# Copies of the strided score operands by GpSimd in a dilated attention layer, with the low part of the probabilities stored over the scores

## The chip, the cores and the metric

The kernel runs on one core of a Trainium2 chip. A core has five engines that run side by side, each in the order of its own instruction stream: TensorE (PE, with its weight loads as PEld), VectorE (DVE), ScalarE (ACT), GpSimd (POOL) and SyncE (SP). They meet at semaphores. DMA transfers are issued from the streams of SP, ACT and POOL. The metric is the device time of one execution in microseconds; less is better. The profile shows one execution with the time of each instruction.

## The reference, cut to what matters

The program is a trunk of two residual layers on 2048 tokens of 1024 columns. The first (even) layer has forgetting attention and gated linear attention, the second (odd) layer retention and dilated attention. Only the dilated attention of the odd layer is touched. It has eight heads of 64 columns, and each head is computed at three dilations:

```python
DIL_PATTERNS = ((128, 1), (512, 4), (2048, 16))

def _dilated_branch(q, k, v, window, dil):
    span = window // dil
    ...
    qs = to_strided(q)                  # tokens t, t + dil, ... in blocks of 128
    kb = with_prev(to_strided(k))       # a block and the one before it
    vb = with_prev(to_strided(v))
    s = jnp.einsum('bhrnqd,bhrnkd->bhrnqk', qs, kb, preferred_element_type=F32) * dh ** -0.5
    valid = (rel >= 0) & (rel <= span) & (...)
    s = jnp.where(valid, s, -jnp.inf)
    mx = jnp.max(s, axis=-1, keepdims=True)
    p = jnp.exp(s - mx)
    den = jnp.sum(p, axis=-1, keepdims=True)
    o = jnp.einsum('bhrnqk,bhrnkd->bhrnqd', p, vb.astype(F32)) / den
    lse = (mx + jnp.log(den))[..., 0]
```

With dilation 4 the query at t sees t, t - 4, ..., t - 512. With dilation 16 there are 128 tokens in each residue class, so there is one block and none before it. The outputs at the three dilations are mixed by a softmax of their lse.

## The kernel before

Every fp32 operand is kept as two fp16 parts. A head's queries and keys lie in one tile st of 128 partitions x 3 x 2048 tokens: column blocks [q_hi; q_lo], [k_hi; k_hi] and [k_lo; k_lo], so that two matmuls give the whole product of a query block and a key block. Tokens are consecutive in the free direction. A residue class at dilation 4 or 16 is therefore a slice with step 4 or 16 (8 or 32 bytes), used directly as a matmul's operands: slice(512 * b + r, 512 * b + 512, 4) or slice(r, S, 16).

A head has 12 groups of four units; a unit is a query block of 128 tokens with its keys. Groups 0 to 3 are dilation 1 (pattern 0), groups 4 to 7 are dilation 4 (pattern 1, group 4 + b is the block b of 512 tokens with the four residues), groups 8 to 11 are dilation 16 (pattern 2, four residues each). They run in the order 4 to 11, then 0 to 3. A unit has 256 keys where there is a block before it, and 128 otherwise (always in pattern 2).

The function scores works on one group. TensorE makes eight matmuls (lines 873 and 874) into one of two PSUM tiles big. VectorE scales, masks and takes the row maximum of each unit into the fp32 tile raw, named dl_s (line 876, line 879), ScalarE takes the exponential with the row sum (line 880), then rounds the whole group to fp16 as ph (line 882). VectorE subtracts and writes the rest as fp16 pl (line 883). SyncE issues two transposing DMAs, ph and pl into the tile pt (lines 884 and 885). Tiles dl_s, dl_ph, dl_pl and dl_pt have two buffers each. The function values, two groups later (LAG = 2), makes the products of pt with the values (lines 895 and 896) into aux, and ScalarE and VectorE add them up (lines 899 and 902).

Between these steps TensorE makes the projections: those of the next head (Heads.tiles: 48 matmuls of 192 columns through the helper rows, lines 163 to 165, into one of two PSUM tiles dn) and others that are stored to memory (Extra.rows, 256 columns). A projection of the next head is rotated by VectorE (lines 743 to 746) and GpSimd (line 747, the sum), and rounded by ScalarE (line 402 for q and k, line 403 for v) and VectorE (lines 405 and 407). Every four row tiles, SyncE transposes q and k into st of the next head (line 413). GpSimd stores the other projections (x_out, line 233), sends the results of patterns 1 and 2 through memory to put the tokens in their order (rec_d, lines 909 and 910), and loads v in the order of the patterns (lines 840 to 844). Weights are split into two parts by ScalarE and VectorE (lines 82 and 83).

The lists of steps are merged by costs written in the code (merge, periods). A planner then sets each engine's order by a simulated timeline (schedule_with_timeline_sim=True), in which an instruction waits for its buffers. So engine order is not always the order of the text.

Of the kernel before, what the change touches and what calls it, by code (L numbers as in the profile page):

```python
# [7 lines left out]
F32 = mybir.dt.float32  # L8
# [9 lines left out]
S = 2048  # L18
# [7 lines left out]
GLA_BUFS = 2  # rows that a recurrence may run ahead of the output products  # L26
RET_BUFS = 3
RET_ROWS = 3  # rows of retention next to the last of the other products
SHARE1, REST1 = 120.0, 20.0  # products left for the last head's attention, and for after it
SHARE2, REST2 = 80.0, 40.0  # L30
LAG = 2  # steps from scores to values
LAG_EVEN, LAG_ODD = 2, 2  # row tiles from the output's operands to its products


class Core:
    """Tools that both layers share: norms, weights in two fp16 parts, products."""
# [24 lines left out]
    def pow2_scale(self, s, inv, ssq):  # L61
        """Powers of two s and inv = 1 / s with sqrt(ssq) * s < 2**14.5."""
# [7 lines left out]
    def rstd(self, ssq, n, shift, k=1):  # L70
        """2**shift / sqrt(ssq / n + EPS)"""
# [8 lines left out]
    def split(self, hi, lo, x, scale):  # L80
        """hi + lo = x * scale"""
        self.nc.scalar.activation(hi, x, AF.Copy, scale=scale)  # L82
        self.nc.vector.scalar_tensor_tensor(lo, x, scale, hi, op0=OP.mult, op1=OP.subtract)  # L83
# [4 lines left out]
    def put_u(self, u, t, h, work):  # L88
        """Row tile t of the normed stream, split and transposed."""
# [15 lines left out]
    def begin_w(self, into, key, *args):  # L105
        """Load a weight now, and leave the rest of its work to finish_w."""
# [9 lines left out]
    def start_w(self, w, segs, gain, pool=None, space=None):  # L116
        """Columns of a weight times the gain of their rows, in two fp16 parts, and the scale's inverse."""
# [37 lines left out]
    def rows(self, out, u, t, w, c0, c1):  # L155
        """out[token, column] = u[tile t] @ w[:, c0:c1]"""
# [10 lines left out]
    def cols(self, out, u, b, w, c0, c1):  # L167
        """out[column, token] of a block of 512 tokens"""
# [9 lines left out]
def merge(main, fill):  # L178
    """Emit two lists of (cost, unit), the second spread evenly over the first."""
# [13 lines left out]
def take(units, cost):  # L193
    """The first units that come to about a cost, taken off their list."""
# [7 lines left out]
class Extra:  # L202
    """Products that go to memory: silu's two factors, and the operands of the recurrent heads."""
# [16 lines left out]
    def rows(self, n, t, k, store):  # L220
        """Row tiles t and t + 1 of 256 columns."""
# [13 lines left out]
    def cols(self, n, b, c, k, store):  # L235
        """128 columns of a block of 512 tokens."""
# [7 lines left out]
    def units(self, gate0, gate_d, after, rows=(), cols=()):  # L244
        """cols: ((first columns, stores, shifts) of two times 128 columns); rows: (first column, store).
        after: weights to load for later."""
# [31 lines left out]
class Recurrent:  # L278
    """The steps of recurrent heads in their order, and the rows that they made."""
# [921 lines left out]
```

## Time and profile before

| | |
|---|---|
| median of 3 runs | 2428.81 us (2408.69, 2428.81, 2563.56) |
| span of the profiled execution | 2434.8 us |
| busy: TensorE, VectorE, ScalarE, GpSimd | 2208.3, 1579.2, 1166.1, 493.0 us |
| mean granted TensorE clock | 0.955 |
| groups of dilated scores | 96, from 1320.4 to 2108.5 us of the span |

The profiled execution has no time of its own in the list of runs; its span, from first to last instruction, lies 6.0 us above the median. In the profile a row of instructions names its line in the kernel, the engine, the operation, and the tiles written and read. An engine's matmuls overlap, so the distance from one start to the next says what a matmul costs, not its printed length. A wait is put down to the instruction that released it last. [...]

### The profile page before, as it was taken

The page shows a single profiled execution, that of the slowest core. Times are in us where ns is not written, and L with a number is a line of the kernel's source. Part 1 is how long each engine was busy: PE and PEld are TensorE (multiplying, and loading weights), DVE is VectorE, ACT ScalarE, POOL GpSimd, SP SyncE. Part 2 cuts the span into 40 slices and gives each one's busy share as a digit, 9 for nine tenths or more (in the row PEclk, how much of TensorE's full clock was granted, in tenths as well). Part 3 has the DMA queues.
Part 4 walks back from the last instruction along what each step waited for, and adds up shares of the span by engine and source line. Part 5 has one row for each costly group of instructions (what it writes and reads, how often), then busy time and mean ns, then how long its engine had stood idle before and what let it go on. Part 6 is the DMA issues. An engine that isn't in the chain of part 4 may idle for free.

```text
span 2434.8 us, 52412 instructions
## 1 busy us (share of the span) xinstructions
PE 2208.3 (91%) x19956; PEld 1701.8 (70%) x19956; DVE 1579.2 (65%) x5190; ACT 1166.1 (48%) x2772; POOL 493.0 (20%) x510
## 2 busy tenths in 40 slices
PE   5877889798898899999999999999899899899998
PEld 4766768565667788764447888788787787765554
DVE  5456656765657567766557676666675666687774
ACT  5534445444545445544444555455453445633322
POOL 1020111101011111111111231222212122145341
PEclk8899889899999999999999999999999999989999
DMA  9868877878878686898876777885867768866653
GB/s 229 164 123 138 144 134 139 153 133 138 154 127 161 127 151 141 172 258 202 220 194 148 138 148 144 145 177 114 160 123 151 136 130 150 164 220 173 178 173 104
DMA packets 846652, 381.95 MB, mean 157 GB/s; under 512 B 749232, under 2 KB 805440, under 8 KB 846144
## 3 DMA queue, kind: packets, MB, share of 16 engines
q1 hardware_dynamic: 748976, 259.31, 57.2%
q0 software_dynamic: 23584, 82.33, 12.3%
q10 hardware_dynamic: 73840, 36.97, 6.5%
q8 instruction: 156, 2.56, 0.5%
q14 instruction: 96, 0.79, 0.1%
HBM read 135.40 MB, written 73.73 MB: 86 GB/s over the span
## 4 chain that ended last, share of the span: by engine, by line
PE 58%; DMA 22%; DVE 10%; issue 4%; ACT 3%; SPq 2%; POOL 1%; ACTq 0%; POOLq 0%; DVEq 0%
PE dn L163 10%; PE dn L165 10%; PE dn L164 10%; DMA fx_tl<-fx_pl 7%; PE dn L334 3%; PE dn L336 3%; PE dn L335 3%; DMA dl_pt<-dl_pl 3%; PE big L873 2%; PE big L874 2%; DMA w_raw<-in_w_in_even_dram 2%; PE aux L524 2%; PE big L498 2%; DMA fx_th<-fx_ph 1%; PE big L499 1%
## 5 line engine op out<-in xcount | busy, mean ns | idle before, releaser
L163 PE MATMUL dn<-w,uh 128*128 128x192 f16 (+1 forms) x3840 | 1012.2, 264 | 13.1 <-DVE head L407 6.7
L165 PE MATMUL dn<-w,ul 128*128 128x192 f16 (+1 forms) x3840 | 1011.1, 263 | 8.1 <-DMA ul<-u_lo 8.1
L164 PE MATMUL dn<-w,uh 128*128 128x192 f16 (+1 forms) x3840 | 1011.9, 264 | 0.0
L163 PEld LDWEIGHTS <-uh 128*128 128x128 f16 x3968 | 394.7, 100 | 51.6 <-DMA uh<-u_hi 10.9
L165 PEld LDWEIGHTS <-ul 128*128 128x128 f16 x3968 | 393.3, 100 | 42.0 <-DMA ul<-u_lo 14.4
L164 PEld LDWEIGHTS <-uh 128*128 128x128 f16 x3968 | 394.0, 100 | 32.2 <-issue 4.0
L508 ACT ACTIVATE fx_s<-fx_s,fx_nm 128x1664 f32<-128x1664 f32 (+15 forms) x128 | 153.4, 1199 | 163.0 <-DVE fx_nm L507 154.2
L880 ACT ACTIVATE dl_s<-dl_s,dl_m 128x256 f32<-128x256 f32 (+1 forms) x384 | 172.7, 452 | 114.9 <-DVE dl_m L879 99.4
L512 DVE TENSOR_TENSOR fx_pl<-fx_s,fx_ph 128x1664 f16<-128x1664 f32 (+15 forms) x128 | 165.9, 1298 | 92.4 <-ACT fx_ph L511 55.2
L876 DVE CUSTOM_DVE_ANT_0 dl_s<-big,dl_mask,hd_f 128x256 f32<-128x256 f32 (+1 forms) x384 | 141.8, 421 | 58.2 <-PE big L874 57.1
L502 DVE CUSTOM_DVE_ANT_0 fx_s<-big,cb,hd_f 128x1024 f32<-128x1024 f32 (+7 forms) x128 | 133.6, 1046 | 49.6 <-PE big L501 26.5
L511 ACT ACTIVATE fx_ph<-fx_s 128x1664 f16<-128x1664 f32 (+15 forms) x128 | 141.0, 1106 | 51.3 <-DMA fx_th<-fx_ph 45.3
L524 PE MATMUL aux<-head,fx_th 128*128 128x128 f16 x1088 | 125.8, 229 | 43.0 <-DMA fx_th<-fx_ph 41.4
L525 PE MATMUL aux<-head,fx_tl 128*128 128x64 f16 x1088 | 114.6, 201 | 45.9 <-DMA fx_tl<-fx_pl 45.7
L77 POOL TENSOR_TENSOR rs_r<-rs_v,mhalf 128x1 f32<-128x1 f32 (+2 forms) x96 | 71.1, 743 | 389.0 <-DVE rs_v L74 354.9
L883 DVE TENSOR_TENSOR dl_pl<-dl_s,dl_ph 128x512 f16<-128x512 f32 (+2 forms) x96 | 100.4, 1048 | 69.6 <-ACT dl_ph L882 38.8
L524 PEld LDWEIGHTS <-fx_th 128*128 128x128 f16 x1088 | 103.1, 104 | 54.4 <-DMA fx_th<-fx_ph 49.4
L525 PEld LDWEIGHTS <-fx_tl 128*128 128x128 f16 x1088 | 98.3, 102 | 56.7 <-DMA fx_tl<-fx_pl 54.6
L83 DVE SCALAR_TENSOR_TENSOR w<-w_raw,w_gs,w 128x256 f16<-128x256 f32 (+2 forms) x296 | 123.3, 466 | 11.0 <-ACT w L82 10.9
L873 PE MATMUL big<-head 128*128 128x256 f16 (+1 forms) x384 | 129.5, 355 | 0.6 <-DVE dl_rec L876 0.6
L874 PE MATMUL big<-head 128*128 128x256 f16 (+1 forms) x384 | 129.7, 357 | 0.0
L498 PE MATMUL big<-head 128*128 128x512 f16 (+3 forms) x320 | 114.1, 357 | 15.3 <-DVE fx_m L502 13.6
(235 smaller groups left out, 4340.1 us busy)
## 6 DMA issues: line engine op xcount, KB each, us to landing
gate_d<-x_out POOLq DMA_DIRECT2D x64, 256.0 KB, 4.0
o_gate<-gate_d SPq DMA_DIRECT2D x32, 512.0 KB, 4.6
rec_d<-dl_rec POOLq DMA_DIRECT2D x16, 528.0 KB, 5.3
dl_rec<-rec_d POOLq DMA_DIRECT2D x16, 528.0 KB, 6.2
x_h<-in_x_dram SPq DMA_DIRECT2D x16, 512.0 KB, 4.7
cb<-cum_d SPq DMA_DIRECT2D x16, 512.0 KB, 9.5
o_mix<-mix_d SPq DMA_DIRECT2D x32, 256.0 KB, 3.2
o_h<-in_x_dram SPq DMA_DIRECT2D x16, 512.0 KB, 4.6
```

The source lines that it names most:

```text
L163: nc.tensor.matmul(out, uh[:, k, xs], wh[:, k, c0:c1], start=k == 0, stop=False)
L164: nc.tensor.matmul(out, uh[:, k, xs], wl[:, k, c0:c1], start=False, stop=False)
L165: nc.tensor.matmul(out, ul[:, k, xs], wh[:, k, c0:c1], start=False, stop=k == KT - 1)
L498: nc.tensor.matmul(p[:, k0:k1], q, st[:, 1, ks], start=True, stop=False)
L508: nc.scalar.activation(raw[:, :n], raw[:, :n], AF.Exp, bias=nm[:, 0:1], accum_out=nm[:, 1:2])
L512: nc.vector.tensor_sub(pl[:, :n], raw[:, :n], ph[:, :n])
L524: nc.tensor.matmul(pv, th[:, k, :], v[:, k, :], start=k == 0, stop=False)
L525: nc.tensor.matmul(pv[:, 0:64], tl[:, k, :], v[:, k, 0:64], start=False, stop=k == i)
L873: nc.tensor.matmul(p[:, sp], st[:, 0, qs], st[:, 1, ks], start=True, stop=False)
L874: nc.tensor.matmul(p[:, sp], st[:, 0, qs], st[:, 2, ks], start=False, stop=True)
L876: nc.vector.tensor_tensor_reduce(out=raw[:, sp], in0=p[:, sp], in1=mask[:, 256 - 128 * len(vs):], scale=f[:, 0:1], scalar=-3.0e38, op0=OP. ...
L880: nc.scalar.activation(raw[:, sp], raw[:, sp], AF.Exp, bias=m[:, i:i + 1], accum_out=rec[:, n, 65:66])
```

## The change

The strided operands of patterns 1 and 2 are no longer read by the matmuls. For each group 4 to 11 a new function stage has GpSimd copy the four residues (three column blocks x 4 residues x 128 tokens) out of st into a tile dl_g with contiguous tokens. dl_g has two buffers. The copy for group g + 1 is asked for behind the matmuls of group g (stage(h, g + 1)); that of a head's first group, 4, where its own scores begin. In pattern 1 the keys lie in two staged tiles (this block and the one before), so each pair of matmuls with 256 keys becomes two pairs with 128. Pattern 0 reads st as before.

To make room, pl is written over the scores (both is one tile with two buffers, seen as fp32 for the scores and as fp16, in its first half, for pl), and ph has one buffer instead of two. All else in the diff takes comments away.

```diff
-            out.append((1, [(4 * b + r, slice(512 * b + r, 512 * b + 512, 4),
-                             slice(512 * max(b - 1, 0) + r, 512 * b + 512, 4),
+            out.append((1, [(4 * b + r, None, None,
                              [v2[:, k, r, :] for k in ((b - 1, b) if b else (0,))]) for r in range(4)]))
...
+    def stage(h, g):
+        if (h, g) in staged or g not in range(4, 12):
+            return
+        st = heads.st[h]
+        src = (st[:, :, 512 * (g - 4):512 * (g - 3)].rearrange("p s (i r) -> p s r i", r=4) if g < 8
+               else st.rearrange("p s (i r) -> p s r i", r=16)[:, :, 4 * (g - 8):4 * (g - 7), :])
+        staged[h, g] = work.tile([128, 3, 4, 128], F16, name="dl_g")
+        nc.gpsimd.tensor_copy(staged[h, g], src)
...
+        stage(h, g)
         p = co.ps([128, 1024], "big")
-        raw = work.tile([128, 1024], F32, name="dl_s")
-        ph = work.tile([128, 1024], F16, name="dl_ph")
-        pl = work.tile([128, 1024], F16, name="dl_pl")
+        both = work.tile([128, 2048], F16, name="dl_s")
+        raw, pl = both.bitcast(F32), both[:, 0:1024]
+        ph = work.tile([128, 1024], F16, name="dl_ph", bufs=1)
...
-            nc.tensor.matmul(p[:, sp], st[:, 0, qs], st[:, 1, ks], start=True, stop=False)
-            nc.tensor.matmul(p[:, sp], st[:, 0, qs], st[:, 2, ks], start=False, stop=True)
+            if pat == 0:
+                nc.tensor.matmul(p[:, sp], st[:, 0, qs], st[:, 1, ks], start=True, stop=False)
+                nc.tensor.matmul(p[:, sp], st[:, 0, qs], st[:, 2, ks], start=False, stop=True)
+                continue
+            j = n % 4
+            for i in range(len(vs)):
+                ks = staged[h, g - len(vs) + 1 + i]
+                kp = slice(sp.start + 128 * i, sp.start + 128 * (i + 1))
+                nc.tensor.matmul(p[:, kp], staged[h, g][:, 0, j, :], ks[:, 1, j, :], start=True, stop=False)
+                nc.tensor.matmul(p[:, kp], staged[h, g][:, 0, j, :], ks[:, 2, j, :], start=False, stop=True)
+        if pat and g < 11:
+            stage(h, g + 1)
```

## Rows read from the trace of the kernel before

**Rows 1.** The page's first part: busy us, share of the span and instructions.
```profile
PE 2208.3 (91%) x19956; PEld 1701.8 (70%) x19956; DVE 1579.2 (65%) x5190; ACT 1166.1 (48%) x2772; POOL 493.0 (20%) x510
```

**Rows 2.** By stretch: PE, PEld, DVE, ACT, POOL busy us; clock, DMA share, GB/s.
```profile
1320.00:2130.00 810.00, 758.23 (x7695) 668.72 (x7693) 535.43 (x2227) 414.94 (x1275) 191.74 (x204) 0.97 0.76 144
1320.00:1724.00 404.00, 393.18 (x4089) 351.72 (x4087) 275.89 (x1164) 213.44 (x656) 97.60 (x107) 0.99 0.76 146
1724.00:2130.00 406.00, 365.05 (x3609) 317.00 (x3607) 259.54 (x1063) 201.50 (x621) 94.14 (x97) 0.94 0.76 141
```

**Rows 3.** Waits of TensorE, 1320 to 2130: total us, times, longest.
```profile
PE aux L895 <- DMA dl_pt<-dl_ph: 24.1, 4, 10.1
PE aux L896 <- DMA dl_pt<-dl_pl: 23.8, 10, 4.7
...
PE dn L163 <- DVE x_out L230: 0.6, 2, 0.5
```

**Rows 4.** Timeline of TensorE at 1740: start, length, instruction, idle before it.
```profile
1740.04 0.29 PE L895 MATMUL aux<-head,dl_pt 128*128 128x128 f16 x1 [6.49 <-DMA dl_pt<-dl_ph]
```

**Rows 5.** Table by stretch behind that wait, columns as in rows 2.
```profile
1742.00:1745.50 3.50, 3.50 (x20) 2.50 (x18) 0.99 (x5) 3.23 (x11) 1.89 (x1) 0.50 0.00 0
```

**Rows 6.** Four score groups by stretch, line 873 alone: PE, PEld, clock, DMA.
```profile
1754.77:1756.60 1.83, 1.62 (x4) 0.44 (x4) 1.00 0.38 87
1766.50:1768.39 1.89, 1.66 (x4) 0.51 (x4) 1.00 0.91 182
1724.68:1725.61 0.93, 0.93 (x4) 0.39 (x4) 1.00 1.38 107
1401.58:1402.35 0.77, 0.77 (x4) 0.37 (x4) 1.00 1.03 360
```

**Rows 7.** GpSimd's groups by form, whole span: count, busy us, mean ns, idle.
```profile
L474 POOL TENSOR_SCALAR cb<-cb,hd_f 128x1024 f32<-128x1024 f32 x16 | 50.2, 3139 | 183.2 <-DMA cb<-cum_d 156.2 <-DVE qk_x L405 16.4 <-DVE fx_nm L526 10.6
L933 POOL TENSOR_TENSOR dl_rec<-dl_rec,dl_es 128x1024 f32<-128x1024 f32 x24 | 47.5, 1997 | 37.6 <-DVE dl_es L930 15.0 <-DVE dl_m L879 12.1 <-ACT dl_s L880 4.3
```

**Rows 8.** Waits of GpSimd, 1320 to 2130.
```profile
POOL qkv_d L233 <- ACT x_out L232: 85.4, 19, 9.1
POOL dl_rec L910 <- DMA rec_d<-dl_rec: 47.4, 11, 13.2
```

**Rows 9.** Timelines of VectorE and GpSimd, 2060 to 2069.
```profile
2063.11 4.07 DVE L883 TENSOR_TENSOR dl_pl<-dl_s,dl_ph 128x1024 f16<-128x1024 f32 x2 [0.52 <-ACT dl_ph L882]
...
2059.48 6.62 POOL L933 TENSOR_TENSOR dl_rec<-dl_rec,dl_es 128x1024 f32<-128x1024 f32 x3 [0.40 <-ACT dl_s L880]
```

**Rows 10.** Instructions on tile dl_s: ns shortest/median/longest, first and last start.
```profile
L876 DVE CUSTOM_DVE_ANT_0 dl_s<-big,dl_mask,hd_f x384: 335/474/490, 1331.0 to 2112.5; 128x256 f32<-128x256 f32 x112, 128x128 f32<-128x128 f32 x80
...
L883 DVE TENSOR_TENSOR dl_pl<-dl_s,dl_ph x96: 681/1212/2922, 1339.5 to 2120.0; 128x1024 f16<-128x1024 f32 x48, 128x512 f16<-128x512 f32 x40, 128x896 f16<-128x896 f32 x8
```

**Rows 11.** Timeline of ScalarE around 1486, a projection of the next head.
```profile
1485.66 0.28 ACT L403 ACTIVATE head<-dn 128x128 f16<-128x128 f32 x1
1486.53 0.42 ACT L402 ACTIVATE qk_x<-dl_r 128x256 f16<-128x256 f32 x1 [0.60 <-POOL dl_r L747]
```

**Rows 12.** Timelines of VectorE and SyncE, one group at stride 16.
```profile
1487.34 0.35 DVE L876 CUSTOM_DVE_ANT_0 dl_s<-big,dl_mask,hd_f 128x128 f32<-128x128 f32 x1 [1.22 <-PE big L874]
...
1495.13 1.28 SPq L885 DMA_TRANSPOSE dl_pt<-dl_pl  x1
```

**Rows 13.** Lines 884 and 885 alone: shortest/median/longest from issue to landing.
```profile
DMA to landing us min/median/max: 2.4/3.6/17.5
...
DMA to landing us min/median/max: 2.4/4.2/20.1
```

**Rows 14.** Waits of SyncE's queue, 1320 to 2130.
```profile
SPq L884 <- PE aux L896: 153.5, 45, 12.6
```

**Rows 15.** Waits of all engines, 1320 to 2130, VectorE and ScalarE for transposes.
```profile
DVE dl_pl L883 <- DMA dl_pt<-dl_pl: 30.5, 6, 16.0
...
ACT dl_ph L882 <- DMA dl_pt<-dl_ph: 27.9, 9, 14.3
```

More of the change, by code (lines that the diff above doesn't have):

```diff
@@ L835, in dilated @@
     nc.sync.dma_start(mask, cst["c_dmask"])
-    recs, live = {}, {}
+    recs, live, staged = {}, {}, {}
     def groups(h):
@@ L850, in groups @@
         for b in range(4):
-            out.append((1, [(4 * b + r, slice(512 * b + r, 512 * b + 512, 4),
-                             slice(512 * max(b - 1, 0) + r, 512 * b + 512, 4),
+            out.append((1, [(4 * b + r, None, None,
                              [v2[:, k, r, :] for k in ((b - 1, b) if b else (0,))]) for r in range(4)]))
         for r0 in range(0, 16, 4):
-            out.append((2, [(r, slice(r, S, 16), slice(r, S, 16), [v3[:, r, :]]) for r in range(r0, r0 + 4)]))
+            out.append((2, [(r, None, None, [v3[:, r, :]]) for r in range(r0, r0 + 4)]))
         recs[h] = [keep.tile([128, NT, 66], F32, name=f"dl_rec{i}", bufs=2 if i == 1 else 1) for i in range(3)]
         return out
+    def stage(h, g):
[6 more added lines that the diff above has]
+        nc.gpsimd.tensor_copy(staged[h, g], src)
     def scores(h, g, pat, units):
         rec, st, f = recs[h][pat], heads.st[h], heads.f[h]
+        stage(h, g)
         p = co.ps([128, 1024], "big")
-        raw = work.tile([128, 1024], F32, name="dl_s")
-        ph = work.tile([128, 1024], F16, name="dl_ph")
-        pl = work.tile([128, 1024], F16, name="dl_pl")
+        both = work.tile([128, 2048], F16, name="dl_s")
+        raw, pl = both.bitcast(F32), both[:, 0:1024]
+        ph = work.tile([128, 1024], F16, name="dl_ph", bufs=1)
         pt = work.tile([128, 2, 8, 128], F16, name="dl_pt")
```

## The prediction, made before the result

> **What bounds the kernel now.** I read the page's first part first [rows 1]: TensorE is busy 91% of a span of 2434.8 us, VectorE 65%, ScalarE 48%, GpSimd 20%. That is a mean over stages, so the second view is the table by stretch [rows 2]. The change touches only the part in which the dilated heads run, 1320 to 2130 us. There TensorE is busy 758 of 810 us, VectorE 535, ScalarE 415, GpSimd 192, at a granted clock of 0.97. The two halves differ: in 1320 to 1724 TensorE is idle 11 of 404 us, in 1724 to 2130 it is idle 41 of 406 and the clock is lower. Third, who TensorE waits for there [rows 3]: almost only for the transposed probabilities, 24.1 us for the high part and 23.8 us for the low part in 14 waits. It hardly ever waits for the accumulators dn (0.6 us). So the stage is set by TensorE's own work, plus a few late transposes, and a microsecond taken from TensorE is worth a microsecond as long as the other engines keep up.
>
> [...]
>
> **What the contiguous operands remove.** A group of scores is eight matmuls (lines 873 and 874). Four stretches of one group each at clock 1.00 give its price [rows 6]: stride 4 with 256 columns 1.83 us, stride 16 with 128 columns 1.89 us, stride 4 with 128 columns (first block of a head) 0.93 us, stride 1 in its mixed first group 0.77 us. That last one has six matmuls of 256 columns and two of 128, 1792 columns: 0.77 / 14 = 0.055 us for each 128 columns. At stride 4 it is 1.83 / 16 = 0.114 us, at stride 16 it is 1.89 / 8 = 0.236 us. The same columns thus take 2.1 and 4.3 times as long. After the change every one of these matmuls is 128 columns of contiguous operands, and I take 0.055 us for each. A full stride-4 group has 16 of them (each 256-column product is cut in two, because its keys lie in two tiles): 0.88 us. The other two kinds have eight: 0.44 us. By the code the 96 groups of eight heads are 24, 8 and 32 of the three kinds and 32 at stride 1. The gain on TensorE is 24 x (1.83 - 0.88) + 8 x (0.93 - 0.44) + 32 x (1.89 - 0.44) = 22.8 + 3.9 + 46.4 = 73 us. Its lower bound, if the 192 additional matmuls cost 0.11 us like a 256-column one, is 73 - 192 x 0.055 = 62 us.
>
> [...]
>
> **What the copies cost.** 64 GpSimd copies of 128 x 1536 fp16 come in. The trace has no copy on GpSimd. Its nearest rows [rows 7] are the product of 1024 elements with a broadcast in 1997 ns (1.95 ns an element) and the one-input multiplication of 1024 in 3139 ns (3.07). So one copy costs 3.0 to 4.7 us; I take 3.7, because a copy has one input like the dearer row but less arithmetic. All 64 are 190 to 300 us on an engine that is busy 192 of 810 us: GpSimd does not become the bound by its load.
>
> [...]
>
> TensorE now waits for the copy. The copy of group g + 1 is queued behind the matmuls of group g (two buffers dl_g, and group g still reads the other). A group comes every 810 / 96 = 8.4 us, 7.7 us after the gain; less the matmuls that leaves about 7 us for a copy of 3.7, so most copies are covered by the projections between the groups. The cover fails where GpSimd's queue stands: it waits 85.4 us in 19 waits before stores of x_out, and 47.4 us in 11 waits (longest 13.2) for the landing of rec_d [rows 8]. A copy that the planner put behind one of these comes 4 us late or more. The first copy of a head has no group ahead of it that requests it, but can go early, since its source is long there. I put 15 us on TensorE for both: eight heads with one late copy of about 2 us. The bounds are 0 (all covered) and 64 x 2.7 us (below).
>
> VectorE pays too. Two subtractions of line 883 took 4.07 us together beside three GpSimd products that run then [rows 9]; one of them is the longest of all, 2.92 us, where the median is 1.21, while line 876, which reads the scores in PSUM, never takes more than 0.49 [rows 10]. So an instruction of VectorE with two SBUF inputs (lines 883, 83 and 405) waits for a running GpSimd one. If three copies in four hold one such instruction up for half their length, 1.4 us a copy, this is 90 us of waiting on an engine that is busy 535 of 810. It lengthens the way from scores to transposes, which has slack in the first half; 5 us on TensorE, bounds 0 and 40. The rotary addition behind a copy delays line 402 on ScalarE, yet not the release of dn: line 403 reads the accumulator ahead of it [rows 11].
>
> **What the smaller buffers cost.** The low part is now written over the scores, so the two buffers dl_s are held until the low part has been transposed, not until the subtraction; ph has one buffer and is held until its transpose has landed. The example at stride 16 [rows 12] runs from its first score at 1487.34 to the issue of the low transpose at 1495.13. With a median landing of 4.2 us [rows 13] that is 12.0 us for one of two buffers, 6.0 us a group: below 7.7. For ph it is the writing, which I take as long as the subtraction's 1.2 us, and 3.6 us to landing, 4.8 us: below 7.7 too. But SyncE holds the high transpose back 45 times, 153.5 us in all, until TensorE has read the old pt [rows 14], 3.4 us each, and then ph's hold is 8.2 us; and the longest landings are 17.5 and 20.1 us. In these cases ScalarE stands at line 882 or VectorE at line 876, in order, with x_out, head and the exponentials queued behind, and the accumulators dn are released late. Today's waits of this kind (27.9 us at line 882, 30.5 us at line 883, [rows 15]) will grow. Since pt is still two groups deep, TensorE sees only what exceeds a group's time: I put 20 us; bounds 0 and 75 (every one of the 45 loses half of its 3.4 us, at TensorE's price).
>
> **Sum.** -73 + 15 + 5 + 20 = -33 us of 2434.8. That execution's span lies 6 us above the median of the runs, 2428.8, of which one is at 2408.7; I carry the share over: 2428.8 - 33 = 2396 us, 1.4% faster.
>
> **Rivals.** (a) The whole gain arrives: the planner moves the copies to where GpSimd is idle, and a faster TensorE releases pt earlier, so transposes go earlier. For it: TensorE's idle of only 11 us in the first four heads. Against: 41 us of idle in the last four, where it waits for transposes that the change does not hasten. 2428.8 - 50 to -73: 2356 to 2379 us.
> (b) The gain is given back at the buffers: ScalarE and VectorE stand for landings, and TensorE's 73 us become waits for pt and dn. For it: a hold of 8.2 us against a period of 7.7 in 45 of 96 groups. Then 73 against 75: 2425 to 2440 us.
> (c) Slower: GpSimd's ordered queue becomes TensorE's clock. A copy of 4.7 us behind one standing store (85.4 / 19 = 4.5 us) ends 9.2 us after the group before, where the next group wants it at about 6.5 us; it decides as soon as copy and queue exceed that 6.5. If all 64 come 2.7 us late it is 173 us, less 73: 2530 us; if half as many plus some time at the lower clock, 2480 us. For it: GpSimd waits in order nearly all the time it is idle. Against: at the planner's hand the copies are ready before the stores that follow the same group.
> (d) The stride isn't what slows these matmuls, and nothing is gained: then the copies and the 192 additional matmuls cost 10 to 30 us. The four stretches of equal clock speak against it.
>
> **How the numbers follow.** Forecast 0.37 (2385 to 2415), (a) 0.25, (b) 0.16, (c) 0.19, (d) 0.03. A measurement of this kernel tells about 2% from no change, 2380 to 2477 us. Faster by more than 2% is (a) and a little of the forecast, 0.29; slower is (c) and a part of (b) with a lower clock, 0.22; within is the rest, 0.49. The range takes in (a) but for its end, the forecast, (b) and the milder half of (c): 2354 to 2482.
>
> **What would show it.** Right: scores that start 0.055 us apart, a span of lines 873 and 874's groups of 0.44 and 0.88 us, copies of 3 to 4.7 us, TensorE's busy time in the stage down by some 70 us and its idle time up by some 40, mostly before values (transposes) and a little before the scores (GpSimd). Wrong towards faster: idle time that does not grow. Wrong towards slower: TensorE idle before scores with GpSimd as releaser in most groups, or ScalarE's line 882 standing for landings for more than 100 us with dn waits on TensorE behind it, and a granted clock below 0.95 in the stage.

## The result, and the profile after it

The changed kernel takes 2538.65 us (median of 4 runs, 2533.39 to 2544.49), the kernel before 2429.91 us. The ratio is 1.0458, with a 95% interval of 1.0394 to 1.0521: slower by 109 us. The ratio leaves out the one execution of the kernel before that took 2563.56 us. The prediction was 2396 us with a range from 2354 to 2482.

The page's first part, after: busy time and share of the span.

```profile
PE 2187.7 (86%) x20148; PEld 1699.4 (67%) x20148; DVE 1652.4 (65%) x5190; ACT 1162.6 (46%) x2772; POOL 638.6 (25%) x574
```

Against [rows 1], TensorE has 21 us less to do, VectorE 73 us more, GpSimd 146 us more. The table by stretch says where the time is, columns as in [rows 2]: first the kernel before, then the changed one, each cut at its last product with the values.

```profile
1320.00:2139.00 819.00, 767.23 (x7785) 676.85 (x7783) 541.82 (x2250) 416.94 (x1279) 193.93 (x206) 0.97 0.76 143
2139.00:2435.00 296.00, 276.87 (x1527) 154.90 (x1523) 209.85 (x597) 95.58 (x181) 125.62 (x105) 0.95 0.59 171
```

```profile
1320.00:2226.00 906.00, 750.42 (x8073) 677.45 (x8070) 606.34 (x2231) 413.01 (x1275) 346.74 (x274) 0.93 0.67 133
2226.00:2539.00 313.00, 270.95 (x1350) 146.67 (x1347) 213.21 (x589) 91.97 (x175) 120.16 (x98) 0.88 0.51 151
```

The stage that took 819 us takes 906. In it TensorE is idle 156 us, against 52 before, and its clock is 0.93, not 0.97. What follows takes 313 us in place of 296, at a clock of 0.88. It begins with a single wait of 16.2 us, longer than any in the stage, for the first rotary sum of the retention; in the kernel before its longest wait for such a sum is 1.6 us.

```profile
2242.39 0.90 PE L786 MATMUL aux<-ident,rt_r 128*128 128x128 f32 x3 [16.16 <-POOL rt_r L747]
```

Two groups of scores after, first line of each pair alone (columns PE, PEld, clock, DMA share, GB/s), with stride 4 and 16 in the source:

```profile
1777.16:1778.05 0.89, 0.89 (x8) 0.73 (x8) 1.00 0.71 146
1816.51:1816.96 0.45, 0.45 (x4) 0.31 (x4) 1.00 1.04 357
```

They answer to the first two of [rows 6], 1.83 and 1.89 us. Of the 24 full stride-4 groups, 23 take 0.89 us, and 33 of the 40 others 0.45: what the prediction said, 0.88 and 0.44. So the matmuls are as fast as forecast, and the loss is in waiting and in the lower clock. TensorE's waits from 1320 to 2240 (total us, times, longest), for [rows 3]:

```profile
PE aux L915 <- DMA dl_pt<-dl_ph: 64.4, 27, 14.4
PE aux L916 <- DMA dl_pt<-dl_s: 51.5, 30, 5.4
PE dn L163 <- DVE head L407: 22.6, 9, 6.2
PE dn L163 <- DVE x_out L230: 6.5, 4, 2.8
```

48 us of waiting for transposes have become 116, and dn, which cost 0.6 us, costs 29. A GpSimd copy is not among TensorE's waits at all. The copies, by form (mean ns, then what ended GpSimd's idle time before them), and on the tile (shortest/median/longest):

```profile
L866 POOL COPY dl_g<-head 128x1536 f16<-128x1536 f16 x64 | 146.2, 2300 | 84.8 <-PE big L892 45.3 <-DMA head<-qk_x 21.6 <-issue 15.9
...
L866 POOL COPY dl_g<-head x64: 1534/2508/3224, 1343.6 to 2166.0; 128x1536 f16<-128x1536 f16 x64
```

They are shorter than the 3.0 to 4.7 us taken from [rows 7]: mean 2.30 us. The waits of ScalarE and VectorE in the same stretch:

```profile
ACT dl_s L900 <- DVE dl_m L899: 177.8, 80, 11.8
...
ACT dl_ph L902 <- DMA dl_pt<-dl_ph: 58.7, 20, 13.2
DVE dl_s L896 <- DMA dl_pt<-dl_s: 57.3, 23, 11.1
DVE dl_s L896 <- PE big L892: 51.5, 30, 7.6
```

Lines 902 and 896 stand for transposes as forecast, 58.7 and 57.3 us where [rows 15] have 27.9 and 30.5. The last line, VectorE waiting for the scores, turns out to be the clue. In the kernel before it is 57.1 us, beside scores that take 1.8 us a group. Beside contiguous operands, with the smaller buffers and without copies, it is short (kernel e3_bufs_contig, below):

```profile
DVE dl_s L876 <- PE big L874: 9.7, 8, 2.3
```

One place shows what a copy does to VectorE. The timelines of VectorE, GpSimd and ScalarE at 1916 (start, length, and in brackets the idle time before it):

```profile
1916.39 2.99 DVE L405 SCALAR_TENSOR_TENSOR qk_x<-dl_r,qk_x 128x128 f16<-128x128 f32 x1
1919.30 0.20 DVE L899 TENSOR_SCALAR dl_m<-dl_rec 128x1 f32<-128x1 f32 x2
...
1916.19 3.04 POOL L866 COPY dl_g<-head 128x1536 f16<-128x1536 f16 x1
...
1919.47 0.51 ACT L900 ACTIVATE dl_s<-dl_s,dl_m 128x256 f32<-128x256 f32 x1 [2.37 <-DVE dl_m L899]
```

Line 405, whose median is 0.28 us, lasts 2.99 us, to within 0.15 us of the copy's end. The small line 899 behind it comes late, and an exponential stands 2.37 us for it.

### The profile page after: what moved, and what is told of

Same layout as the page of the kernel before. It is cut to its first block, busy times and chain, and to the rows that moved or that the text cites. A ratio compares the mean times of both kernels' runs of the same rounds, so it can differ in the third digit from the quotient of the medians.

```text
span 2539.0 us, 52900 instructions
## 1 busy us (share of the span) xinstructions
PE 2187.7 (86%) x20148; PEld 1699.4 (67%) x20148; DVE 1652.4 (65%) x5190; ACT 1162.6 (46%) x2772; POOL 638.6 (25%) x574
## 4 chain that ended last, share of the span: by engine, by line
PE 40%; DMA 29%; DVE 16%; ACT 7%; issue 5%; SPq 2%; POOL 1%; ACTq 0%; DVEq 0%; POOLq 0%
DMA dl_pt<-dl_s 6%; DMA fx_tl<-fx_pl 6%; PE dn L163 6%; PE dn L165 6%; PE dn L164 6%; DMA dl_pt<-dl_ph 4%; DVE dl_s L896 3%; PE dn L334 2%; PE dn L336 2%; PE dn L335 2%; DMA fx_th<-fx_ph 2%; DVE w L83 2%; ACT dl_s L900 2%; PE aux L524 2%; DMA w_raw<-in_w_in_odd_dram 2%
## 5 line engine op out<-in xcount | busy, mean ns | idle before, releaser
L163 PE MATMUL dn<-w,uh 128*128 128x192 f16 (+1 forms) x3840 | 1022.7, 266 | 45.6 <-DVE head L407 29.4
L165 PE MATMUL dn<-w,ul 128*128 128x192 f16 (+1 forms) x3840 | 1022.1, 266 | 7.7 <-DMA ul<-u_lo 7.7
L164 PE MATMUL dn<-w,uh 128*128 128x192 f16 (+1 forms) x3840 | 1022.6, 266 | 0.0
L165 PEld LDWEIGHTS <-ul 128*128 128x128 f16 x3968 | 398.7, 101 | 40.4 <-DMA ul<-u_lo 11.8
L896 DVE CUSTOM_DVE_ANT_0 dl_s<-big,dl_mask,hd_f 128x256 f32<-128x256 f32 (+1 forms) x384 | 140.9, 420 | 109.2 <-DMA dl_pt<-dl_s 57.3
L866 POOL COPY dl_g<-head 128x1536 f16<-128x1536 f16 x64 | 146.2, 2300 | 84.8 <-PE big L892 45.3
L511 ACT ACTIVATE fx_ph<-fx_s 128x1664 f16<-128x1664 f32 (+15 forms) x128 | 140.8, 1105 | 51.5 <-DMA fx_th<-fx_ph 44.5
L903 DVE TENSOR_TENSOR dl_s<-dl_s,dl_ph 128x512 f16<-128x512 f32 (+2 forms) x96 | 110.6, 1152 | 75.8 <-ACT dl_ph L902 75.2
L83 DVE SCALAR_TENSOR_TENSOR w<-w_raw,w_gs,w 128x256 f16<-128x256 f32 (+2 forms) x296 | 130.1, 487 | 10.2 <-ACT w L82 10.0
L233 POOL DMA_DIRECT2D gate_d<-x_out x64 | 46.3, 724 | 324.6 <-DVE x_out L230 187.6
```

Source lines behind the costliest of these rows:

```text
L163: nc.tensor.matmul(out, uh[:, k, xs], wh[:, k, c0:c1], start=k == 0, stop=False)
L164: nc.tensor.matmul(out, uh[:, k, xs], wl[:, k, c0:c1], start=False, stop=False)
L165: nc.tensor.matmul(out, ul[:, k, xs], wh[:, k, c0:c1], start=False, stop=k == KT - 1)
L511: nc.scalar.activation(ph[:, :n], raw[:, :n], AF.Copy)
L866: nc.gpsimd.tensor_copy(staged[h, g], src)
L896: nc.vector.tensor_tensor_reduce(out=raw[:, sp], in0=p[:, sp], in1=mask[:, 256 - 128 * len(vs):], scale=f[:, 0:1], scalar=-3.0e38, op0=OP. ...
```

## The experiments

Three numbers are worked out from each trace. "Way": the columns of projections (lines 163 to 165) that stand in TensorE's order between a group's last score and its first value product, at 2400 columns a us (a fixed conversion; in the kernel before, at clock 1.00, 24 matmuls of 192 columns take 1.98 us from 1341.34 on, 2330 columns a us), median of the 96 groups. It is the work under which the chain of maxima, exponentials and transposes must fit. "Values" and "dn": TensorE's idle time just ahead of value products and of projections, from the first dilated score to the last value product, whatever released it.

| kernel | us | ratio to before, 95% interval | way | values | dn |
|---|---|---|---|---|---|
| before | 2429.91 | | 14.1 | 49 | 1 |
| e1_contig | 2385.16 | 0.9750 to 0.9839 | 14.1 | 73 | 3 |
| e2_bufs | 2455.7 | 1.0064 to 1.0121 | 14.1 | 42 | 4 |
| e3_bufs_contig | 2421.25 | 0.9926 to 0.9984 | 14.1 | 56 | 11 |
| e10_short | 2434.21 | 0.9960 to 1.0034 | 14.1 | 63 | 12 |
| e13_half | 2450.11 | 1.0054 to 1.0116 | 14.1 | 70 | 32 |
| e9_bystander | 2464.78 | 1.0067 to 1.0187 | 14.1 | 46 | 55 |
| e20_memset | 2427.56 | 0.9984 to 1.0062 | 14.1 | 57 | 15 |
| e21_two_memsets | 2436.87 | 0.9983 to 1.0051 | 14.1 | 84 | 12 |
| e22_four_memsets | 2519.96 | 1.0286 to 1.0386 | 11.4 | 123 | 10 |
| e14_fixed | 2523.17 | 1.0305 to 1.0405 | 9.4 | 119 | 29 |
| e4_copies_strided | 2523.85 | 1.0288 to 1.0416 | 9.6 | 48 | 37 |
| the changed kernel | 2538.65 | 1.0394 to 1.0521 | 9.1 | 118 | 34 |
| e7_act | 2462.94 | 1.0054 to 1.0172 | 14.1 | 84 | 13 |
| e8_dve | 2504.64 | 1.0194 to 1.0345 | 14.1 | 78 | 11 |
| e12_rec1 | 2567.39 | 1.0519 to 1.0601 | 13.0 | 135 | 41 |
| e11_ahead | 2595.06 | 1.0635 to 1.0722 | 14.3 | 101 | 72 |
| e15_text_before | 2553.38 | 1.0457 to 1.0549 | 14.1 | 42 | 3 |
| e16_text_contig | 2546.57 | 1.0442 to 1.0498 | 14.1 | 59 | 26 |
| e17_text_after | 2618.63 | 1.0724 to 1.0803 | 12.8 | 42 | 42 |

The kernel before was run again beside each round of experiments. Its medians there lie between 2427.91 and 2434.66 us, so a difference of a few us between kernels of different rounds says nothing. For the first round, e1 to e4, it was 2432.69 us.

**Each part alone.** e1_contig is the kernel before with contiguous slices in place of the strided ones (first diff; stride 4 likewise), e2_bufs the one with the smaller buffers (second diff), e3_bufs_contig has both. e4_copies_strided is the changed kernel whose queries come from the copies and whose keys are strided slices of st.

```diff
-            out.append((2, [(r, slice(r, S, 16), slice(r, S, 16), [v3[:, r, :]]) for r in range(r0, r0 + 4)]))
+            out.append((2, [(r, slice(128 * r, 128 * r + 128), slice(128 * r, 128 * r + 128), [v3[:, r, :]]) for r in range(r0, r0 + 4)]))
```

```diff
-        raw = work.tile([128, 1024], F32, name="dl_s")
+        both = work.tile([128, 2048], F16, name="dl_s")
+        raw, pl = both.bitcast(F32), both[:, 0:1024]
+        ph = work.tile([128, 1024], F16, name="dl_ph", bufs=1)
```

> The kernel before, but at dilations 4 and 16 the matmuls of the scores read 128 or 256 consecutive tokens of st in place of every 4th or 16th: the gain of contiguous operands alone, without copies and with the buffers of before. It leaves out the right choice of tokens, so the attention at those two dilations is computed on others. Both theories expect the scores at 0.055 us for 128 columns and 50 to 73 us less, 2357 to 2380 us. If it is less than 30 us faster, TensorE's time was not what sets the stage, and the gain was never there.

> The kernel before with strided operands and no copies, but with the low part written over the scores and one buffer ph. Theory B (the buffers are the loss): 90 to 180 us slower than before, 2520 to 2610 us, with VectorE waiting at the row maximum for the transpose of the low part and ScalarE at ph. Theory C (GpSimd's copies are the loss, by holding VectorE and by making TensorE's order later): at most 30 us slower, 2430 to 2460 us.

> The smaller buffers and contiguous operands without any copy (consecutive tokens of st, so other tokens are attended at dilations 4 and 16). The changed kernel less its copies. Theory B: 2490 to 2550 us, nearly the changed kernel's 2539, as TensorE's gain does not come through. Theory C: 2360 to 2400 us, as in the run without smaller buffers.

> The changed kernel with all its copies and its smaller buffers, where the queries are read from the copies and the keys from st with stride 4 or 16, so TensorE waits for each copy and reads slowly as before. Against the run with smaller buffers alone it adds the copies. Theory B: within 30 us of that run. Theory C: 80 to 150 us above it.

Contiguous operands alone give 48 us of the 73 forecast (2433 - 2385); TensorE's wait for transposes rises from 49 to 73 us. The buffers cost 23 us alone and 36 beside contiguous operands (2421 - 2385). The profiled executions of e1_contig and e3_bufs_contig differ by 9 of these 36 us only. In them the stage from first score to last value product is as long (782 and 781 us), and the loss stands behind it. The stretch behind, in e1_contig and then in e3_bufs_contig:

```profile
2096.00:2391.00 295.00, 279.17 (x1517) 155.80 (x1515) 209.74 (x594) 95.63 (x181) 124.96 (x104) 0.95 0.58 172
```

```profile
2086.00:2401.00 315.00, 282.93 (x1469) 156.85 (x1465) 207.61 (x592) 94.10 (x180) 122.16 (x102) 0.89 0.54 160
```

Both parts together still gain 11 us. So the copies cost 2538.65 - 2421.25 = 117 us, and with strided keys, where they bring nearly nothing, still 68 (over e2_bufs). The prediction put them at 20. e1_contig lies 5 us above its expected range, and e3_bufs_contig and e4_copies_strided lie between the ranges of the two theories, so neither theory held as it stood. In e4_copies_strided, with contiguous queries and strided keys, the full groups still take 1.80 us at stride 4 and 1.83 us at stride 16 (medians, from one start to the next), so the price of the stride lies with the keys.

**Which property of the copies.** e10_short copies 96 of the 1536 elements, e13_half 768, e14_fixed all; these three use two fixed tiles (first diff, e10_short). e9_bystander is e3_bufs_contig with the whole copies made and read by VectorE's one-element copy alone, so that no matmul waits for them (second diff).

```diff
-        nc.gpsimd.tensor_copy(staged[h, g], src)
+        staged[h, g] = two[g % 2]
+        nc.gpsimd.tensor_copy(staged[h, g][:, :, :, 0:8], src[:, :, :, 0:8])
```

```diff
+        if pat:
+            nc.vector.tensor_copy(junk, staged[h, g][:, 0, 0, 0:1])
```

> The changed kernel with each copy cut to 96 of its 1536 elements (8 tokens of each residue), in two fixed tiles zeroed once; every matmul still reads a staged tile and so depends on its copy. It leaves out 15 of 16 parts of the copies, so the scores at dilations 4 and 16 are mostly zero. Theory L: within 25 us of the run without copies, 2410 to 2445 us. Theory P: close to the changed kernel, 2500 to 2540 us. In between, in the proportion to the copies' length, both.

> The run with smaller buffers and contiguous operands without copies (2421 us), plus GpSimd's 64 copies at the changed kernel's pace, with the matmuls not reading them: VectorE reads one element of each copy (64 instructions of about 0.1 us) so that the copies come group by group. As in that run other tokens are attended at dilations 4 and 16. It tells the copies' length (they hold VectorE and GpSimd's queue) from TensorE's dependence on them. Theory L (length): 60 to 110 us above 2421, 2480 to 2530 us. Theory P (TensorE must wait for each copy, or its order is planned around them): at most 30 us above it, 2420 to 2450 us.

> The run with short copies, with 768 of 1536 elements in each copy (64 of 128 tokens of a residue; the rest of a tile stays zero, so scores at dilations 4 and 16 are partly left out). Theory R: the order depends on how long the planner takes a copy to be; with half of it the cover between scores and values is 13 us or more and the time at most 20 us above the short copies', 2435 to 2460 us; or, if half is still too long for the plan, the cover is 9 us and the time is over 2480 us, which theory R would also have to show in TensorE's waits. Theory L: halfway between short and whole copies, 2475 to 2500 us, at any cover.

> The runs with short and half copies, with the copies whole: the changed kernel with two fixed tiles in place of the rotating pair, nothing left out. Its cover between scores and values is 9.4 us in TensorE's order, as in the changed kernel (9.1), where half copies have 14.1. Theory O (from half to whole copies the planner's order changes and that costs): 2515 to 2545 us, 65 us or more above half copies. Theory L (length alone, about 16 us for each further half as from short to half): 2460 to 2480 us. If it is near the changed kernel, the rotating pair as such has no part in the loss.

To depend on a copy costs TensorE 13 us when the copy is short, with the 192 additional matmuls. Whole copies that no matmul waits for cost 43, between the ranges of the two theories. Half copies cost 29, whole ones 102: the jump lies between half and whole, and there the way falls from 14.1 to 9.4 us. The pair of buffers is not the cause, as e14_fixed stays near the changed kernel.

What the 43 us of e9_bystander are, its waits of TensorE against those of e3_bufs_contig show (1320 to 2200):

```profile
PE aux L895 <- DMA dl_pt<-dl_ph: 29.1, 13, 4.8
PE aux L896 <- DMA dl_pt<-dl_s: 22.9, 11, 5.3
...
PE dn L163 <- DVE head L407: 4.0, 4, 1.9
```

```profile
PE dn L163 <- DVE head L407: 27.5, 13, 5.5
PE aux L912 <- DMA dl_pt<-dl_s: 26.7, 17, 5.5
PE dn L163 <- DVE x_out L230: 19.2, 9, 5.1
```

The second is e9_bystander: the transposes cost no more, dn does. Line 405, the one with two SBUF inputs ahead of line 407 in VectorE's order, in e3_bufs_contig and then in e9_bystander (shortest/median/longest ns):

```profile
L405 DVE SCALAR_TENSOR_TENSOR qk_x<-dl_r,qk_x x116: 271/282/1982, 1325.3 to 1989.2; 128x128 f16<-128x128 f32 x116
```

```profile
L405 DVE SCALAR_TENSOR_TENSOR qk_x<-dl_r,qk_x x116: 272/285/3449, 1325.2 to 2056.3; 128x128 f16<-128x128 f32 x116
```

Its mean rises from 310 to 529 ns; all lines with two SBUF inputs or a copy between SBUF tiles (405, 410, 411, 83 and the low part) take 261 us instead of 215 in the stage, 410 instructions each. Two other ways are closed: VectorE's one-element copy never stands for a copy in e9_bystander, and ScalarE's waits for the rotary sums behind the copies in GpSimd's queue (1320 to 2240) do not grow, in e3_bufs_contig and then in e9_bystander:

```profile
ACT qk_x L402 <- POOL dl_r L747: 27.7, 25, 6.6
```

```profile
ACT qk_x L402 <- POOL dl_r L747: 16.2, 17, 2.7
```

**GpSimd at work, but reading nothing.** e20_memset is e9_bystander with two memsets for each copy; e21_two_memsets and e22_four_memsets are the changed kernel with two and four memsets of dl_g for each copy, read by the matmuls.

```diff
-        nc.gpsimd.tensor_copy(staged[h, g], src)
+        nc.gpsimd.memset(staged[h, g], 0.0)
+        nc.gpsimd.memset(staged[h, g], 0.0)
```

> The run with copies that no matmul reads, with each copy replaced by two memsets of the same tile on GpSimd: GpSimd's queue is filled at the same places, but it reads nothing from SBUF. VectorE's reading of one element for the pace stays. As in that run other tokens are attended at dilations 4 and 16. Theory H (a GpSimd copy holds up VectorE's instructions with two SBUF inputs, so dn is released late): at most 20 us above the run without copies, 2415 to 2445 us, VectorE's two-input instructions as long as before (line 405 at 0.29 to 0.32 us, 0.53 beside the copies) and TensorE's waits for dn back from 55 to about 10 us. Theory Q (the rotary additions and stores stand behind the copies in GpSimd's queue): 2450 to 2480 us, with those waits.

> The changed kernel with each copy replaced by two GpSimd memsets of the same tile, so that the score matmuls still wait for GpSimd and read the tile, but nothing of the kernel's data is read by GpSimd (the dilated scores of strides 4 and 16 are then of zeros, that part of the computation is left out). A memset took 1.38 us before, so two are 2.8 us, longer than a copy's 2.30. In TensorE's order 14.1 us of projections (median) stand between a group's scores and its values, as in the kernel without copies; in the changed kernel it is 9.1. If whole copies cost what they cost because GpSimd's work is long and TensorE depends on it, this kernel lies near the changed one, 2500 to 2540 us. If it is the holding of VectorE or the planned order, neither of which is here, it lies near the kernel with copies of 96 elements, 2425 to 2450 us.

> The same with four memsets for each copy, about 5.5 us a group (the strided scores are of zeros here too). This changes the planned order as the whole copies did: the projections between a group's scores and its values fall to a median of 11.4 us over all groups, and to 6.4 to 9.3 in five of the eight groups with copies (5.7 to 9.9 in the changed kernel). GpSimd still reads none of the kernel's data, so VectorE isn't held. If the planned order is worth the some 60 us that neither short copies nor unread ones show, this kernel is at 2470 to 2510 us, with waits for transposes near the 116 us of the changed kernel and few for GpSimd. If the order is worth nothing and the holding does it all, it stays at 2425 to 2455 us. If TensorE waits for GpSimd's last memset in many groups (over 20 us in its waits), the run says nothing on the order.

e20_memset costs 6 us. Its memsets, read by nobody but VectorE, ran ahead, all between 1302 and 1597, so they were not where e9_bystander's copies were. In e21_two_memsets they are spread over the stage. Its tile dl_g, its waits from 1320 to 2240 and its line 405:

```profile
L866 POOL MEMSET dl_g<- x64: 1368/1378/1398, 1307.1 to 2069.5; 128x1536 f16 x64
L867 POOL MEMSET dl_g<- x64: 1367/1386/1479, 1310.0 to 2072.8; 128x1536 f16 x64
```

```profile
PE aux L917 <- DMA dl_pt<-dl_s: 44.8, 21, 8.7
...
PE aux L916 <- DMA dl_pt<-dl_ph: 34.2, 19, 4.5
...
PE dn L163 <- DVE head L407: 7.3, 5, 2.8
...
DVE dl_s L897 <- PE big L893: 5.8, 4, 3.9
```

```profile
L405 DVE SCALAR_TENSOR_TENSOR qk_x<-dl_r,qk_x x118: 270/282/1983, 1322.0 to 2029.8; 128x128 f16<-128x128 f32 x118
```

Its 2.76 us a group are longer than a copy and the matmuls depend on them, and it costs 16 us over e3_bufs_contig, with line 405 and dn as without copies. So neither GpSimd's load nor TensorE's dependence on it is the price, up to this length.

The memsets do hold VectorE elsewhere, which the expectation of e22_four_memsets does not allow for: at its copies between two SBUF tiles, lines 410 and 411. Line 411 in e3_bufs_contig and in e21_two_memsets, then line 410 in e22_four_memsets:

```profile
L411 DVE COPY qk_x<-qk_x x30: 209/218/764, 1322.7 to 1991.8; 128x256 f16<-128x256 f16 x30
```

```profile
L411 DVE COPY qk_x<-qk_x x30: 208/244/6931, 1322.6 to 2032.3; 128x256 f16<-128x256 f16 x30
```

```profile
L410 DVE COPY qk_x<-qk_x x31: 214/471/4153, 1323.8 to 2080.6; 128x256 f16<-128x256 f16 x31
```

The one of 6.93 us ends at 1760.19, within 0.1 us of the end of a memset. Lines 410 and 411 together take 15 us without GpSimd's added work, 14 beside the copies of e9_bystander, 39 beside two memsets and 52 beside four. What a held instruction costs thus depends on what stands behind it: here dn is not late. Now e22_four_memsets, its waits, its line 405, and its stretch from 1320 to 2130 in the table by stretch:

```profile
PE aux L918 <- DMA dl_pt<-dl_ph: 76.3, 30, 12.8
...
DVE dl_s L899 <- PE big L895: 45.2, 24, 10.6
...
PE aux L919 <- DMA dl_pt<-dl_s: 40.3, 22, 6.0
...
PE aux L786 <- POOL rt_r L747: 16.4, 1, 16.4
...
PE dn L163 <- DVE head L407: 5.9, 4, 2.1
...
PE big L894 <- POOL dl_g L869: 1.5, 2, 0.9
```

```profile
L405 DVE SCALAR_TENSOR_TENSOR qk_x<-dl_r,qk_x x122: 273/284/1986, 1323.4 to 2080.4; 128x128 f16<-128x128 f32 x122
```

```profile
1320.00:2130.00 810.00, 688.29 (x7498) 627.86 (x7497) 531.75 (x2062) 375.81 (x1168) 502.80 (x435) 0.93 0.70 133
```

Line 405 is not held, dn is not late, and TensorE waits 1.5 us for memsets. Yet this kernel loses 83 us against the one with two, where lines 410 and 411 take 13 us less; it also lies 10 us above the expected range. It has nearly the planned order of the changed kernel. Behind a group of stride 4 or 16, on average 1.4 later groups have their scores ahead of its values in TensorE's order; in the changed kernel it is 1.5, and in the planned kernels of the table with a way of 13.0 or more 2.1 to 2.7. So VectorE waits 45.2 us for scores and TensorE 117 us for transposes, as after the change (51.5 and 116). GpSimd is busy 503 of 810 us here, against 358 with two memsets, and what its other work loses by that is in the 83 us too. Two places can be read: ScalarE's waits for the rotary sums of the heads stay the same (27.0 and 26.0 us), and the wait for the retention's rotary sum behind the stage is 16.4 us in place of 5.4. So the order costs at most some 70 us here; no run changes the order alone.

The orders show that the planner sets scores later behind GpSimd work from some length on. It did not for two memsets of together 2.76 us, and did for a copy of 2.30: it seems to take the copy to be longer than it is. That is inferred from the orders, not measured.

**The copies on another engine.**

```diff
-        nc.gpsimd.tensor_copy(staged[h, g], src)
+        nc.scalar.activation(staged[h, g], src, AF.Copy)
```

e8_dve has nc.vector.tensor_copy in the same place.

> The changed kernel with the 64 copies made by ScalarE in place of GpSimd; ScalarE is busy 415 of 810 us in the stage and takes about 1.4 us for 1536 elements by its row for 1024 in 0.95 us. If holding VectorE is the loss (a part of theory L): 2430 to 2470 us. If TensorE's dependence on a copy is (theory P), whatever engine makes it: 2500 us or more.

> The changed kernel with the 64 copies made by VectorE, in about 1.7 us each by its rows of 1024 elements in 1.22 us, 110 us on an engine busy 535 of 810 us. Holding falls away, but VectorE's own time rises more than GpSimd's copies lengthen it (75 us in the changed kernel). Theory L: 2450 to 2510 us, below the changed kernel. Theory P: 2520 us or more.

On ScalarE the copies cost 42 us over e3_bufs_contig instead of 117. The way is 14.1 us again and dn 13, but now TensorE does wait for copies, and the transposes come later:

```profile
PE aux L916 <- DMA dl_pt<-dl_s: 42.7, 20, 8.8
PE aux L915 <- DMA dl_pt<-dl_ph: 40.9, 24, 6.4
PE big L891 <- ACT dl_g L866: 16.0, 13, 2.9
```

It is the fastest complete version of the change, and 1.1% slower than the kernel before. A copy takes 1.55 to 3.04 us on ScalarE, not the expected 1.4; ScalarE's rows of 1024 elements in the kernel before take 1.05 us or more, not 0.95. VectorE, which has less time to spare (busy 557 of 810 us in e3_bufs_contig, ScalarE 417), costs twice as much (83 us).

**The order by itself.** e11_ahead asks for the copies two groups ahead with three buffers dl_g (first diff), paid for by one buffer of dl_rec1 in place of two; e12_rec1 is its control, the changed kernel with that one buffer alone. In e15_text_before, e16_text_contig (of e3_bufs_contig) and e17_text_after the planner's timeline is off (second diff) and the text sets the order.

```diff
-        if pat and g < 11:
-            stage(h, g + 1)
+        if pat and g < 10:
+            stage(h, g + 2)
```

```diff
-    with tile.TileContext(nc, schedule_with_timeline_sim=True) as tc:
+    with tile.TileContext(nc, schedule_with_timeline_sim=False) as tc:
```

> The changed kernel with each copy asked for two groups ahead in place of one, with three buffers dl_g; the memory comes from one buffer in place of two for the results of dilation 4 (dl_rec1). Theory R (TensorE's order: with a copy asked for one group ahead the planner puts the scores later, so that only 9.1 us of projections stand between a group's scores and its values, against 14.1 before): this cover comes back to 13 us or more, TensorE waits less for the transposes, and the time falls to 2450 to 2485 us, the level of the copies nobody waits for. Theory L (the copies' length alone, whatever the order): 2510 to 2550 us, as in its control.

> Control for the run with copies two groups ahead: the changed kernel with one buffer for the results of dilation 4, all else as it is. Both theories: 2530 to 2560 us, a cover of 9 us as in the changed kernel.

> The kernel before with the planner's timeline switched off, so that instructions stand nearly in the order of the text in all engines; cover 14.1 us. It is the base for the two other runs in this order. Expected 2430 to 2560 us.

> Smaller buffers and contiguous operands without copies (other tokens are attended at dilations 4 and 16), without the planner's timeline; cover 14.1 us. Both theories: near the base in this order, from 30 us less to 20 us more.

> The changed kernel without the planner's timeline; cover 12.8 us, the copies in the order of the text. Theory O (half of the loss by the copies is the order that the planner makes around them): 30 to 70 us above the run without copies in the same order, against 117 with the planner. Theory L (the copies' length and TensorE's dependence, whatever the order): 100 to 130 us above it.

In the order of the text the copies cost 72 us, not 117, with a way of 12.8 us, just above the expected 30 to 70. There the forecast's rival (c) exists:

```profile
PE big L891 <- POOL dl_g L866: 37.5, 11, 6.8
PE dn L163 <- DVE head L407: 26.3, 13, 4.5
```

TensorE stands 37.5 us for copies. In the planned order this wait is gone, and waits for transposes stand in its place. e11_ahead is a miss: it brought the way back to 14.3 us and took 28 us more than its control. The control missed its expectation too (2530 to 2560 us and a way of 9): its way had grown to 13.0 without the copies being moved, and yet it waits longer for values than the changed kernel, 135 us. Both have more waiting for dn (72 and 41 us) than the changed kernel. One buffer of dl_rec1 alone costs 29 us, and why the longer way does not pay beside it stays open. e4_copies_strided does not fit either: it has a way of 9.6 us, but waits only 48 us for values, and what grows is dn (37 us against 4 in e2_bufs). So the way alone does not set the time.

## Why the prediction was wrong

- **Price of the stride: right.** 0.89 and 0.45 us a group as forecast, no cost for the 192 additional matmuls. At stride 4 a full group took 1.83 us before and takes 0.89 after, at stride 16 1.89 and 0.45.
- **"A microsecond taken from TensorE is worth a microsecond": over-sized.** Of 73 us 48 arrive (e1_contig). The rest becomes waiting for transposes, which the change does not hasten: what the text named against rival (a).
- **Smaller buffers, 20 us: right in size, the place not shown.** 23 us alone, 36 beside the faster scores, within the bounds of 0 and 75. The working had the loss in the stage, at buffers held too long; beside contiguous operands the profiles, which show a part of the loss, have it behind the stage (315 us against 295). Why stays open, so the size may be luck. SyncE's wait for pt, 153.5 us in [rows 14] and the lever of the working, is down to 15.3 us in the view of its waits after: the transposes now wait for their sources.
- **Copies and TensorE, 15 us: the step that failed.** The working asked only whether a copy is ready when its scores come. It is: no wait of TensorE in the changed kernel is for a copy. And yet the copies cost 117 us, with the 5 us that were put on VectorE. In place of that wait the planned order has the scores later, the way falls from 14.1 to 9.1 us, and the waits for transposes grow from 48 to 116 us. An order like it, made by memsets that leave line 405 and dn alone, costs up to some 70 us (e22_four_memsets against e21_two_memsets, with more load on GpSimd). In the changed kernel the order's part is only had by difference, some 60 us: 117 less 13 for short copies and some 40 for the holding; the parts need not add up exactly. That it is the order is argued, not shown: e12_rec1, e11_ahead and e4_copies_strided do not follow the way.
- **Copies and VectorE, 5 us: mis-sized.** The holding is as foreseen from [rows 9, 10]: VectorE's lines grow by some 46 us in e9_bystander (90 us of waiting were assumed, and the copies are shorter). But its price on TensorE is 37 to 43 us, not 5 (e9_bystander against e20_memset and e3_bufs_contig), about the upper bound of 40. It came by the way that the working excluded with [rows 11]: dn is released late. Line 403 reads dn ahead of line 402, yet the next reader is line 407, which stands behind line 405 on VectorE. In the changed kernel the longest of lines 83 and 405 are 3.21 and 3.06 us, where their medians are 0.48 and 0.28. Line 405 ends with the copy at 1916, and beside two memsets, which read nothing, its longest is 1983 ns, as without copies (1982).
- **Rival (c): its sign, not its mechanism.** GpSimd's queue never became TensorE's clock in the changed kernel. The test given for it, idle time ahead of scores with GpSimd as releaser, did not come up; the other, a clock below 0.95 with line 902 standing, did in part (0.93, though 58.7 us, not over 100).
- **Length of a copy: too high.** 2.30 us on average, under the lower bound of 3.0, with medians of 1.58 us at stride 4 and 2.98 us at stride 16.

Copies beside the old, larger buffers were not tried.

## What to carry to other kernels

When a planner sets the order, an added producer that is never waited for may still set the pace: compare the order of the consumer's engine, and how much independent work is left under the chain behind it, before looking for waits on the producer. Here a GpSimd copy was also charged to VectorE's two-input instructions (line 405's mean went from 310 to 529 ns) and to whoever waited behind them, so follow VectorE's queue to the release of each PSUM buffer. Test a new stage with a substitute of like length that reads nothing (memsets), then with the real one. Then check what the substitute itself holds: the memsets here left line 405 alone (median 0.28 us, longest 1.98) but held VectorE's copies between SBUF tiles (up to 6.93 us), and four of them changed the order too.

## What was not expected of the hardware

- A strided copy of 128 x 1536 fp16 costs about the same on three engines: 1534 to 3224 ns on GpSimd, 1547 to 3037 on ScalarE, 1736 to 2970 on VectorE (shortest and longest in the changed kernel, e7_act and e8_dve). On GpSimd the copies at stride 4 are the short ones (median 1.58 us) and those at stride 16 the long ones (2.98). GpSimd is not the slow one for it.
- 64 copies of 2.35 us on average that no matmul waits for cost 43 us of time, and the granted clock from 1320 to 2130 falls from 0.95 (e3_bufs_contig) to 0.92; 128 memsets of 1.38 us that the matmuls depend on cost 16 us at 0.96.
- GpSimd's memsets, which read nothing, held VectorE's copies between SBUF tiles: one of line 411, whose median is 0.22 us without them, took 6.93 us beside four memsets in e21_two_memsets.
- The stride's price lies with the keys: with contiguous queries and strided keys a full group takes 1.80 us (stride 4) and 1.83 us (stride 16), against 1.83 and 1.89 us with both strided.
